# Weight blocks loaded between the parts of the memory input, their products channel by channel, and small operations queued behind later work, in a two-block transformer layer

## The chip, the cores and the metric

The kernel runs on one core of a Trainium2 chip (trn2). The metric is the device time of one execution in microseconds (us). Five engines work beside each other, each on its own queue of instructions: TensorE (PE) multiplies matrices, VectorE (DVE) and ScalarE (ACT) work element by element, GpSimd (POOL) and SyncE (SP) mainly start transfers (DMA) between the chip's memory and the core's buffers. An engine takes its instructions strictly in the order of its queue; semaphores make one engine wait for another.

## The reference

`x` (256 tokens x 1024) and a memory `mem` (256 x 1024) go through two blocks, in float32. The first block:

```python
h = rms_norm(x, norm_g); mem_h = rms_norm(mem, mem_norm_g)
(c_glu, c_gate, d_q, d_k, d_v, d_gate, x_q, x_gate, merge) = split(h @ w_in)
y_conv = conformer_conv_branch(c_glu, c_gate, ...)            # GLU, 31-tap depthwise conv, layer norm, silu, projection
y_diff = differential_attention_branch(d_q, d_k, d_v, d_gate, ...)   # 8 heads, two softmaxes subtracted
k, v = split(mem_h @ w_mem_kv); y_mem = memory_cross_attention_branch(x_q, x_gate, k, v, ...)
g = sigmoid(merge)
x = x + (g[0] * y_conv + g[1] * y_diff + g[2] * y_mem) @ w_out
```

The second block has stick-breaking attention (8 heads of 64) beside a gated linear recurrence (RG-LRU, 512 channels, whose decay is `exp(-8 r softplus(-lambda))`), a projection `w_out_2`, and a PEER feed-forward: for every token 8 heads pick 16 of 128 x 128 experts by product keys, and sum `gelu(h . u_e) v_e` over them.

## The kernel before

**The stream of weights.** All weights of both blocks are laid out as 94 blocks of 1 MB in the order of their use (`STREAM`). A block arrives as two halves `raw` (128 x 1024 each, 512 KB, five buffers) on SP's queue. `prep` (L235) loads both halves and splits each into a high part `whi` (a cast on ACT, L248) and a low part `wlo` (a subtraction on DVE, L249), four buffers each. A product with float32 accuracy then takes three matmuls (high by high, high by low, low by high), so a block is 48 matmuls of 128x256 on PE. `block` hands out a prepared block, `ahead` (L262 on) prepares exactly one block ahead. The result of a block is a tile `lin` in PSUM, three buffers. `linN` (L332 to 347) computes with the activations as the stationary side, first all channels of tokens 0 to 127, then all of tokens 128 to 255; `linT` (L309 to 311) the other way round.

**The order of the blocks.** Blocks 0 to 3 make the memory's values (`linN`), 4 to 11 the conv branch's GLU, 12 to 15 the cross attention's gate, 16 to 19 the memory's keys, 20 to 23 its queries, 24 to 31 the differential attention's queries and keys, 32 to 39 its values and the cross attention's projection, 40 to 43 its gate (`gated`, L661 on), 44 to 47 and 48 to 59 the merge gates (`merge_gate`, L674 on) and the projection between them, 60 to 67 the conv branch's end, 68 to 71 `w_out`, 72 to 81 the second block's input projection, 82 to 85 `w_out_2`, 86 to 93 the PEER queries. Behind them 64 + 64 blocks of expert matrices `u` and `v` are read whole for most tokens (L290, L1187), while the experts of 96 rows (token slots) are gathered one by one with indirect transfers from POOL (L1196, `gat`) and multiplied on DVE (L1203, L1221).

**The front** (L479 to 505). SP issues one part of the memory (`m_t`, four parts of 256 KB), the small vectors `VT`, the other three parts, the two halves of block 0, then `x` (`xr`, two halves of 512 KB), the constants `CT` and `ident`, and then the halves of the blocks from 1 on. `gain_col` (L412 to 415) makes the scaled memory `mgh` (ACT) and its low part `mgl` (DVE) for each of 8 channel groups. `rms_sq` (L437 to 441) squares two groups at a time on ACT and adds them over the channels with two matmuls against ones (8 in all) into `stat`, a PSUM tile of one buffer. `rstd_of` (L373 to 382) turns that sum into 1/sqrt in seven steps (`rv`, `rs`, `rs`, `rt` on ACT, two on DVE), and `tok_scalar` (L418 to 424) turns it into one number per token, `rmt`, by which the results of blocks 0 to 3 are scaled as they leave PSUM (`vm`, L505). Behind block 0 the program asks for the normalised input: `rms_cols` (L430) squares `x` on ACT (L393), adds on DVE (L397), sums by four matmuls into the same `stat` tile (L399), runs `rstd_of`, and makes for each of the 8 channel groups `nrm` (DVE, L409), its high part `hh` (ACT, L386) and its low part `hl` (DVE, L386). Blocks 4 to 15 need these.

**Small operations.** L511 to 517 are six DVE operations on a few columns: scaled gains (`GT`) and products (`lp`) whose first use is block 20 on, except `lp`, which a small matmul (L519) sums for `le` (L521). L769 to 775 prepare the recurrence's decay from `lambda`: on ACT `Abs`, `Exp` and `Ln` (`la`), on DVE `lb`, a sum and two scalings; first used in block 72 on. ACT needs a table load (`ACT_TABLE_LOAD`) where the next function is not in the loaded set; the one that the program loads at its start holds `Exp` and `Ln`.

**What sets the order.** The program is written in the order of use; a scheduler then orders each engine's queue from its own model of the durations. `tc.issue_after(i)` puts an operation behind `i` in that order (`hold`, `background` and `table` use it); a change in one place can so move operations elsewhere. `state["sub"]` is the latest `wlo` subtraction, `state["gate"]` the latest Sigmoid of `merge_gate`.

Of the kernel before, what the change touches and what calls it, by code (L numbers as in the profile page):

```python
# [9 lines left out]
F32 = mybir.dt.float32  # L10
# [9 lines left out]
P = 128  # L20
# [168 lines left out]
def build(tc, xT, memT, vec, con, con0, wcat, rgw, keysT, u, v, urow, vrow, out):  # L189
    nc = tc.nc  # L190
    es = ExitStack()
    with es:
# [42 lines left out]
        def prep(i):  # L235
# [4 lines left out]
            for a in range(2):  # L240
                raw = spool.tile([P, 1024], F32, name="raw", bufs=5)
                nc.sync.dma_start(raw, srcs[i][:, a * 1024:(a + 1) * 1024])
# [89 lines left out]
        def linN(act):  # L332

            ah, al = act
            hs, ls = block()
            ps = lin_ps[0].tile([P, 2, T], F32, name="lin")
            for t in range(2):
                for c in range(8):
                    wh = hs[c // 4].rearrange("p (c j) -> p c j", c=4)[:, c % 4]
                    wl = ls[c // 4].rearrange("p (c j) -> p c j", c=4)[:, c % 4]  # L340
                    xh = ah[:, c, t * P:(t + 1) * P]
                    xl = al[:, c, t * P:(t + 1) * P]
                    nc.tensor.matmul(ps[:, t], xh, wh, start=c == 0, stop=False)  # L343
                    nc.tensor.matmul(ps[:, t], xh, wl, start=False, stop=False)  # L344
                    nc.tensor.matmul(ps[:, t], xl, wh, start=False, stop=c == 7)  # L345
            ahead()
            return ps
# [118 lines left out]
        with ExitStack() as e1:  # L466
# [15 lines left out]
            nc.sync.dma_start(m_t[:, 0:2], memT[:, 0:2])  # L482
            nc.sync.dma_start(VT, vec)
            for k in range(1, 4):
                nc.sync.dma_start(m_t[:, 2 * k:2 * k + 2], memT[:, 2 * k:2 * k + 2])
            prep(0)
            for k in range(2):
                nc.sync.dma_start(x_t[:, 4 * k:4 * k + 4], xT[:, 4 * k:4 * k + 4])
            nc.sync.dma_start(CT, con)
            nc.sync.dma_start(ident, con0[:, :P])  # L490
            mgh, mgl = bigt("mgh", F32R), bigt("mgl", F32R)
            for c in range(NC):
                gain_col(m_t, "mem_norm_g", mgh, mgl, c)
            rm = smt("rm", T, 1)
            stm = statp()
# [15 lines left out]
            nc.vector.tensor_scalar_mul(GT[:, 0:1], V("diff_qn_g"), 0.125)  # L511
# [816 lines left out]
```

## Time and profile before

| what | value |
|---|---|
| three runs | 1286.37, 1287.76, 1290.27 us |
| median | 1287.76 us |
| profiled execution, its own time | 1290.27 us |
| its span | 1288.5 us (1.8 us lie around it) |
| busy, share of the span | PE 97%, DVE 73%, ACT 35%, POOL 17% |
| chain that ended last, by engine | PE 43%, issue 19%, DMA 18%, DVE 10%, POOL 6%, ACT 3% |

All times in a view count from the span's start. A row of the timeline has start, duration, engine, line, operation, output<-input, the count of equal neighbours joined in it, and in brackets how long the engine was idle before and what ended that. Durations of matmuls overlap: what one costs in a row of them is the distance between two starts. A row of the windows view sums the busy time of each engine over a stretch. The chain follows the last instruction back, at each step to what released it.

### The profile page before, as it was taken

To read this page: it belongs to the slowest core of one execution; us is meant where nothing else is said; L and a number is where in the kernel's file an instruction comes from. 1 tells how busy PE (TensorE), PEld (TensorE's weight loads), DVE (VectorE), ACT (ScalarE), POOL (GpSimd) and SP (SyncE) were. 2 spreads that over 40 slices of the span, in tenths; PEclk is the share of its full clock that TensorE was granted. 3 is DMA by queue.
4 is the path that set the end of the run, shared out by engine and by line. 5 is a ranking of instruction groups with operands and counts; after the bars stand their busy time and mean duration, and the time that the engine had idled before them with its cause. 6 is when DMAs were issued, how large, how long until landed. Compare 5 with 4: busy or idle time off the path is not lost.

```text
span 1288.5 us, 24481 instructions
## 1 busy us (share of the span) xinstructions
PE 1252.9 (97%) x9948; PEld 1211.2 (94%) x9948; DVE 936.7 (73%) x1806; ACT 457.4 (35%) x741; POOL 219.3 (17%) x232
## 2 busy tenths in 40 slices
PE   8999999999999999998999999999999999999995
PEld 7999999989999999977999999999999999999884
DVE  6789988888998776865899874678545876454542
ACT  7545677578646556964432111000100000000001
POOL 0000000000000000002013453222342225333330
PEclk9999999999999999999999999999999999999998
DMA  8555544434565664415677899999999999999994
GB/s 287 191 186 188 168 134 131 122 125 148 164 194 167 188 206 156 154 59 200 236 245 220 298 373 408 408 408 404 378 392 334 352 348 407 409 409 409 409 408 155
DMA packets 94865, 340.76 MB, mean 264 GB/s; under 512 B 10576, under 2 KB 12048, under 8 KB 94624
## 3 DMA queue, kind: packets, MB, share of 16 engines
q1 hardware_dynamic: 65312, 232.73, 51.0%
q0 software_dynamic: 29440, 106.46, 21.6%
q8 instruction: 78, 1.28, 0.4%
q14 instruction: 35, 0.29, 0.1%
HBM read 338.01 MB, written 1.05 MB: 263 GB/s over the span
## 4 chain that ended last, share of the span: by engine, by line
PE 43%; issue 19%; DMA 18%; DVE 10%; POOL 6%; ACT 3%; POOLq 0%; SPq 0%; DVEq 0%; ACTq 0%
DMA gat<-in_vrow,gi 13%; PE lin L310 10%; PE lin L309 10%; PE lin L311 10%; POOL gat L1196 5%; DMA gat<-in_urow,gi 5%; PE lin L343 1%; PE lin L345 1%; PE lin L344 1%; DVE gat L1203 1%; DVE acc L1221 1%; DVE wlo L249 1%; PE stat L461 1%; DVE s L997 1%; ACT whi L248 1%
## 5 line engine op out<-in xcount | busy, mean ns | idle before, releaser
L1187 PE MATMUL y<-ga,w 128*128 128x160 f32 x2048 | 292.9, 302 | 5.2 <-DMA w<-in_v 2.5
L1187 PEld LDWEIGHTS y<-ga,w 128*128 128x128 f32 x2048 | 279.9, 190 | 12.5 <-DMA w<-in_v 11.5
L249 DVE TENSOR_TENSOR wlo<-raw,whi 128x1024 fp32r<-128x1024 f32 x188 | 229.3, 1222 | 64.0 <-ACT whi L248 63.3
L290 PE MATMUL lin<-h3f,w 128*128 128x160 f32 x1888 | 265.4, 300 | 0.0
L290 PEld LDWEIGHTS lin<-h3f,w 128*128 128x128 f32 x1888 | 257.7, 190 | 0.2 <-issue 0.2
L248 ACT CAST whi<-raw 128x1024 fp32r<-128x1024 f32 x188 | 196.2, 1049 | 167.0 <-PE lin L310 125.7
L310 PE MATMUL lin<-hl,whi 128*128 128x256 f32 x704 | 200.2, 284 | 0.0
L311 PE MATMUL lin<-hh,wlo 128*128 128x256 f32 x704 | 199.8, 284 | 0.0
L309 PE MATMUL lin<-hh,whi 128*128 128x256 f32 x704 | 199.7, 284 | 0.0
L1221 DVE SCALAR_TENSOR_TENSOR acc<-gat,cG,acc 128x1024 f32<-128x1024 f32 x94 | 120.7, 1284 | 95.9 <-DMA gat<-in_vrow,gi 95.5
L1203 DVE CUSTOM_DVE_ANT_0 gat<-gat,hrow 128x1024 f32<-128x1024 f32 x96 | 116.1, 1223 | 28.6 <-DMA gat<-in_urow,gi 28.6
L311 PEld LDWEIGHTS lin<-hh,wlo 128*128 128x128 f32 x704 | 132.6, 188 | 2.2 <-issue 1.9
L310 PEld LDWEIGHTS lin<-hl,whi 128*128 128x128 f32 x704 | 132.6, 188 | 1.8 <-issue 1.4
L309 PEld LDWEIGHTS lin<-hh,whi 128*128 128x128 f32 x704 | 132.5, 188 | 1.4 <-issue 1.0
L1196 POOL DMA_INDIRECT gat<-in_urow,gi x96 | 101.5, 1058 | 181.2 <-DVE sG L1203 169.4
L1196 POOL DMA_INDIRECT gat<-in_vrow,gi x96 | 93.8, 977 | 166.1 <-DVE acc L1221 137.8
L1176 ACT ACTIVATE ga<-lin 128x320 f32<-128x320 f32 x64 | 28.0, 438 | 243.8 <-PE lin L290 239.5
L950 POOL DMA_DIRECT2D ga<-in_u x10 | 5.4, 545 | 601.3 <-DMA raw<-in_wcat 597.7
L537 DVE SCALAR_TENSOR_TENSOR cacc<-ub,VT,cacc 128x256 f32<-128x256 f32 x240 | 104.0, 480 | 0.0
L1302 ACT COPY ga<-y 128x160 f32<-128x160 f32 x4 | 1.2, 293 | 251.1 <-PE y L1187 251.1
L1165 DVE SCALAR_TENSOR_TENSOR ga<-gp,ga 128x256 f32<-128x256 f32 (+1 forms) x60 | 29.1, 511 | 63.3 <-PE gp L1154 55.9
L310 PE MATMUL lin<-h3lo,whi 128*128 128x256 f32 x128 | 37.6, 294 | 3.0 <-DVE h3lo L386 3.0
(376 smaller groups left out, 2152.0 us busy)
## 6 DMA issues: line engine op xcount, KB each, us to landing
raw<-in_wcat SPq DMA_DIRECT2D x188, 512.0 KB, 4.1
w<-in_v SPq DMA_DIRECT2D x128, 512.0 KB, 13.6
w<-in_u SPq DMA_DIRECT2D x118, 512.0 KB, 9.8
ga<-in_u POOLq DMA_DIRECT2D x10, 512.0 KB, 10.8
gat<-in_urow,gi POOLq DMA_INDIRECT x96, 8.9
gat<-in_vrow,gi POOLq DMA_INDIRECT x96, 18.8
m_t<-in_memT SPq DMA_DIRECT2D x4, 256.0 KB, 3.9
xr<-in_xT SPq DMA_DIRECT2D x2, 512.0 KB, 9.1
```

The costliest lines, as they stand in the source:

```text
L248: nc.scalar.copy(h, raw)
L249: state["sub"] = nc.vector.tensor_sub(l, raw, h.bitcast(F32))
L290: nc.tensor.matmul(ps[:, a], ws[a][:, c * P:(c + 1) * P], x[:, c], start=c == 0, stop=c == 7)
L309: nc.tensor.matmul(ps[:, a], wh, ah[:, c], start=(a, c) in first, stop=False)
L310: nc.tensor.matmul(ps[:, a], wh, al[:, c], start=False, stop=False)
L311: nc.tensor.matmul(ps[:, a], wl, ah[:, c], start=False, stop=(a, c) in last)
L537: nc.vector.scalar_tensor_tensor(cacc[:, c], s, w, cacc[:, c], op0=ALU.mult, op1=ALU.add)
L1165: state["dve"] = nc.vector.scalar_tensor_tensor(g_[:, :, tl], p_, 1.0 / GSCALE, g_[:, :, tl], op0=ALU.mult, op1=ALU.mult)
L1187: nc.tensor.matmul(yT[c // 2][:, c % 2, :D], ws[a][:, c * P:(c + 1) * P], g[:, a], start=False, stop=i == 63 and (a, c % 2) == (1, 1))
L1196: nc.gpsimd.indirect_dma_start(g, None, src, bass.IndirectOffsetOnAxis(gi[:, 0, k:k + 1].bitcast(U32), 0))
L1203: nc.vector.tensor_tensor_reduce(out=g, in0=g, in1=h, scale=1.0, scalar=0.0, op0=ALU.mult, op1=ALU.add, accum_out=sG[:, k:k + 1])
L1221: state["sum"] = nc.vector.scalar_tensor_tensor(acc[m], g, cG[:, k:k + 1], acc[m], op0=ALU.mult, op1=ALU.add)
```

## The change

The halves of blocks 0 and 1 are loaded among the memory's parts: SP's order becomes `VT`, part 0, block 0's first half, parts 1 and 2, block 0's second half, part 3, both halves of block 1, and only then `x`, `CT`, `ident` and the rest. The memory's statistic is squared for the first two channel groups as before (two matmuls), while the other three pairs are squared and added on DVE into one tile (two additions), with two matmuls behind block 0's products: four matmuls instead of eight. `rstd_of` and `tok_scalar` follow there. Block 0's products go channel by channel, both halves of the tokens for each; in all of `linN` the second and third product change places. The six small operations on `GT` and `lp` are put behind the latest `wlo`, `Abs` and `lb` of the decay behind the latest merge gate.

```diff
+        def prep(i, raws=None, between=None):
...
+                raw = load(i, a) if raws is None else raws[a]
+                if between is not None:
+                    between(a)
...
+            if channelwise:
+                seq = [(t, c) for c in range(8) for t in range(2)]
+                first, last = seq[:1], seq[-1:]
+            else:
+                seq = [(t, c) for t in range(2) for c in range(8)]
+                first, last = [(0, 0), (1, 0)], [(0, 7), (1, 7)]
+            for t, c in seq:
...
+                nc.tensor.matmul(ps[:, t], xh, wh, start=(t, c) in first, stop=False)
+                nc.tensor.matmul(ps[:, t], xl, wh, start=False, stop=False)
+                nc.tensor.matmul(ps[:, t], xh, wl, start=False, stop=(t, c) in last)
...
-            nc.sync.dma_start(m_t[:, 0:2], memT[:, 0:2])
             nc.sync.dma_start(VT, vec)
-            for k in range(1, 4):
-                nc.sync.dma_start(m_t[:, 2 * k:2 * k + 2], memT[:, 2 * k:2 * k + 2])
-            prep(0)
+            m_load(0)
+            raws = [load(0, 0)]
+            m_load(1)
+            m_load(2)
+            raws.append(load(0, 1))
+            m_load(3)
+            raws1 = [load(1, a) for a in range(2)]
             for k in range(2):
                 nc.sync.dma_start(x_t[:, 4 * k:4 * k + 4], xT[:, 4 * k:4 * k + 4])
...
+            stm = statp()
+            msq = [smt("sqs", 512, 1), smt("sq"), smt("sq")]
+            nc.scalar.square(msq[0].rearrange("p (a b) -> p a b", a=2), m_t[:, 0:2])
+            for b in range(2):
+                nc.tensor.matmul(stm[:, :T], ONES, msq[0][:, b * T:(b + 1) * T], start=b == 0, stop=False)
+            m_gains(0)
+            prep(0, raws, lambda a: [gain_col(m_t, "mem_norm_g", mgh, mgl, c) for c in (2, 3, 4, 5)] if a else None)
+            for c in (6, 7):
+                gain_col(m_t, "mem_norm_g", mgh, mgl, c)
+            prep(1, raws1)
+            for k in range(1, 4):
+                q = msq[min(k, 2)]
+                nc.scalar.square(q.rearrange("p (a b) -> p a b", a=2), m_t[:, 2 * k:2 * k + 2])
+                if k > 1:
+                    nc.vector.tensor_add(msq[1], msq[1], q)
...
-            for c in range(0, NC, 2):
-                rms_sq(m_t, stm, c, NC)
-            rstd_of(stm[:, :T], 1.0 / 1024, T, out=rm)
-            rmt = tok_scalar(rm, "rmt")
...
             for j in range(4):
-                ps = linN((mgh, mgl))
+                ps = linN((mgh, mgl), j == 0)
+                if j == 0:
+                    for b in range(2):
+                        nc.tensor.matmul(stm[:, :T], ONES, msq[1][:, b * T:(b + 1) * T], start=False, stop=b == 1)
+                    rstd_of(stm[:, :T], 1.0 / 1024, T, out=rm)
+                    rmt = tok_scalar(rm, "rmt")
...
-            nc.vector.tensor_scalar_mul(GT[:, 0:1], V("diff_qn_g"), 0.125)
...
+            with tc.issue_after(state["sub"].ins):
+                nc.vector.tensor_scalar_mul(GT[:, 0:1], V("diff_qn_g"), 0.125)
...
-            nc.scalar.activation(la, lam, AF.Abs)
+            with tc.issue_after(state["gate"].ins):
+                nc.scalar.activation(la, lam, AF.Abs)
             nc.scalar.activation(la, la, AF.Exp, scale=-1.0)
             nc.scalar.activation(la, la, AF.Ln, bias=1.0)
-            nc.vector.tensor_scalar(lb, lam, 0.0, -1.0, op0=ALU.min, op1=ALU.mult)
+            with tc.issue_after(state["gate"].ins):
+                nc.vector.tensor_scalar(lb, lam, 0.0, -1.0, op0=ALU.min, op1=ALU.mult)
```

The change moves instructions in three places on which the prediction rests. The line numbers of the changed kernel are higher by 6 to 40: the cast `whi` is L254 there, the low part of a split L397, `rv`, `rs`, `rs`, `rt` are L387 to L390, `vm` is L542.

**ACT, the start of the chain that makes the normalised input** (`vm` are blocks 0 to 3 leaving PSUM, `rv` to `rt` the statistic of `x`, `hh` the high parts). Before:

```order
L248 CAST whi<-raw 128x1024 x2
L505 ACTIVATE vm<-lin,rmt 128x256 x2
L248 CAST whi<-raw 128x1024 x2
L376 ACTIVATE rv<-stat,VT 128x256
L377 ACTIVATE rs<-rv 128x256
L378 ACTIVATE rs<-rs 128x256
L379 ACTIVATE rt<-rs 128x256
L248 CAST whi<-raw 128x1024
L505 ACTIVATE vm<-lin,rmt 128x256 x2
```

With the change:

```order
L254 CAST whi<-raw 128x1024 x3
L542 ACTIVATE vm<-lin,rmt 128x256 x4
L254 CAST whi<-raw 128x1024 x2
L542 ACTIVATE vm<-lin,rmt 128x256 x2
L387 ACTIVATE rv<-stat,VT 128x256
L388 ACTIVATE rs<-rv 128x256
L389 ACTIVATE rs<-rs 128x256
L390 ACTIVATE rt<-rs 128x256
L254 CAST whi<-raw 128x1024
```

`rv` stood behind one pair of `vm` (block 0's); now it stands behind three (blocks 0, 1 and 2). On PE the four matmuls that sum the squares of `x` stood inside block 1, and now stand at the end of block 2.

**PE, the end of block 46** (`hh,whi` are its products; `att<-ident,pp` are the transposes of the last differential attention head's probabilities, `sig` their copy to the core's buffers by ACT, `att<-sig,vd` the product with the values). Before:

```order
L643 MATMUL att<-ident,pp 128x128 x2
L309 MATMUL lin<-hh,whi 128x256
L310 MATMUL lin<-hl,whi 128x256
L311 MATMUL lin<-hh,wlo 128x256
...
L646 MATMUL att<-sig,vd 128x256
L647 MATMUL att<-sig,vd 128x128
```

With the change:

```order
L316 MATMUL lin<-hl,whi 128x256
L681 MATMUL att<-ident,pp 128x128 x3
L317 MATMUL lin<-hh,wlo 128x256
L684 MATMUL att<-sig,vd 128x256
L685 MATMUL att<-sig,vd 128x128
L315 MATMUL lin<-hh,whi 128x256
```

Before, the first transpose stood 28 products further ahead still, and 18 products stood between the last two transposes and the product with the values; now one does.

**ACT, the same heads a little earlier** (`gate` is the Silu of the differential attention's gate, `pp,z` the softmax, `sig` the copy after the transposes; `rv`, `rs`, `rs`, `rt` here a head norm's statistic). Before:

```order
L376 ACTIVATE rv<-stat,VT 128x512
L664 ACTIVATE gate<-lin 128x512
L377 ACT_TABLE_LOAD
L377 ACTIVATE rs<-rv 128x512
L378 ACT_TABLE_LOAD
L378 ACTIVATE rs<-rs 128x512
L572 ACTIVATE pp,z<-s,nm 128x128 x2
L379 ACTIVATE rt<-rs 128x512
L645 COPY sig<-att 128x384
```

With the change:

```order
L387 ACTIVATE rv<-stat,VT 128x512
L388 ACT_TABLE_LOAD
L388 ACTIVATE rs<-rv 128x512
L254 CAST whi<-raw 128x1024
L702 ACT_TABLE_LOAD
L702 ACTIVATE gate<-lin 128x512
L610 ACT_TABLE_LOAD
L610 ACTIVATE pp,z<-s,nm 128x128 x2
L389 ACTIVATE rs<-rs 128x512
L683 COPY sig<-att 128x384
```

Between `rv` and `pp,z` stood two table loads and no cast; now stand three and one cast.

## Rows read from the trace of the kernel before

**Rows 1.** Windows: stretch and us; busy of PE, PEld, DVE, ACT, POOL; PEclk, DMA share, GB/s.

```profile
0.00:14.40 14.40, 8.13 (x18) 5.62 (x19) 7.65 (x23) 9.99 (x20) 0.20 (x4) 1.00 0.82 281
300.00:350.00 50.00, 49.90 (x391) 48.06 (x391) 45.15 (x84) 41.30 (x63) 0.00 (x0) 1.00 0.51 159
550.00:600.00 50.00, 47.42 (x357) 41.27 (x356) 26.56 (x44) 24.62 (x38) 1.81 (x4) 1.00 0.27 83
725.00:1250.00 525.00, 518.44 (x4218) 509.01 (x4218) 323.34 (x519) 24.81 (x60) 186.67 (x183) 1.00 0.99 385
```

**Rows 2.** The chain that ended last, its longest pieces: start, us, what.

```profile
2.62 6.30 DMA m_t<-in_memT
...
10.42 2.08 PE stat L441 x4
12.71 1.71 PE stat L441 x4
...
1168.04 18.80 DMA gat<-in_vrow,gi
```

**Rows 3.** Timeline of SP's queue, first us: issue of block 0's two halves.

```profile
3.09 0.91 SPq L242 DMA_DIRECT2D raw<-in_wcat  x2
```

**Rows 4.** DMA issues of the stretch 3.4 to 3.8 us: KB each, us to landing.

```profile
raw<-in_wcat SPq DMA_DIRECT2D x2, 512.0 KB, 7.5
```

**Rows 5.** Timeline of PE, blocks 0, 1 and the start of 4.

```profile
12.51 1.91 PE L441 MATMUL stat<-sq,ONES 128*128 128x256 f32 x4
...
14.43 0.41 PE L345 MATMUL lin<-whi,mgl 128*128 128x256 f32 x1
14.64 0.32 PE L343 MATMUL lin<-whi,mgh 128*128 128x256 f32 x1
...
19.84 0.28 PE L344 MATMUL lin<-wlo,mgh 128*128 128x256 f32 x1
19.96 0.28 PE L345 MATMUL lin<-whi,mgl 128*128 128x256 f32 x1
20.17 0.60 PE L422 MATMUL stat<-ONES,rm 1*128 1x1 f32 x4
20.70 0.39 PE L343 MATMUL lin<-whi,mgh 128*128 128x256 f32 x1
...
22.24 1.02 PE L399 MATMUL stat<-sqs,ONES 128*128 128x256 f32 x4
...
39.08 0.36 PE L309 MATMUL lin<-hh,whi 128*128 128x256 f32 x1
39.28 0.28 PE L310 MATMUL lin<-hl,whi 128*128 128x256 f32 x1
```

**Rows 6.** Timeline of DVE, the front.

```profile
12.89 1.22 DVE L249 TENSOR_TENSOR wlo<-raw,whi 128x1024 fp32r<-128x1024 f32 x1 [0.24 <-ACT whi L248]
...
26.41 0.88 DVE L409 SCALAR_TENSOR_TENSOR nrm<-xr,VT,rs 128x256 f32<-128x256 f32 x2
...
39.97 0.75 DVE L386 TENSOR_TENSOR hl<-nrm,hh 128x256 fp32r<-128x256 f32 x2
```

**Rows 7.** Timeline of ACT, the front.

```profile
5.70 0.19 ACT L769 ACTIVATE la<-VT 128x4 f32<-128x4 f32 x1
5.80 0.89 ACT L414 ACTIVATE mgh<-m_t,VT 128x256 fp32r<-128x256 f32 x2
...
21.73 1.99 ACT L248 CAST whi<-raw 128x1024 fp32r<-128x1024 f32 x2
23.62 0.48 ACT L376 ACTIVATE rv<-stat,VT 128x256 f32<-128x256 f32 x1
```

**Rows 8.** Timeline of ACT, blocks 46 and 47.

```profile
326.24 0.62 ACT L386 CAST odh<-gate 128x512 fp32r<-128x512 f32 x1 [0.93 <-DVE gate L665]
...
328.26 0.48 ACT L645 COPY sig<-att 128x384 f32<-128x384 f32 x1
328.76 1.28 ACT L676 ACT_TABLE_LOAD   x1
330.05 0.60 ACT L676 ACTIVATE sig<-lin 128x512 f32<-128x512 f32 x1
```

**Rows 9.** Timeline of PE, the same stretch.

```profile
327.84 0.38 PE L643 MATMUL att<-ident,pp 128*128 128x128 f32 x2
...
330.17 0.59 PE L646 MATMUL att<-sig,vd 128*128 128x256 f32 x2
```

**Rows 10.** Timeline of ACT around the last merge gate of that kind.

```profile
386.88 1.06 ACT L248 CAST whi<-raw 128x1024 fp32r<-128x1024 f32 x1 [1.76 <-PE lin L310]
```

More of the change, by code (lines that the diff above doesn't have):

```diff
@@ L233, in prep_plain, with load @@
             prepared[i] = ws
-        def prep(i):
+        def load(i, a):
+            raw = spool.tile([P, 1024], F32, name="raw", bufs=5)
+            nc.sync.dma_start(raw, srcs[i][:, a * 1024:(a + 1) * 1024])
+            return raw
+        def prep(i, raws=None, between=None):
             if i >= NW:
@@ L330, in linK, with linN @@
                 yield ps
-        def linN(act):
+        def linN(act, channelwise=False):
             ah, al = act
@@ L336, in linN @@
             ps = lin_ps[0].tile([P, 2, T], F32, name="lin")
[L337 to L345, printed above, removed]
+            if channelwise:
[5 more added lines that the diff above has]
+            for t, c in seq:
+                wh = hs[c // 4].rearrange("p (c j) -> p c j", c=4)[:, c % 4]
+                wl = ls[c // 4].rearrange("p (c j) -> p c j", c=4)[:, c % 4]
+                xh = ah[:, c, t * P:(t + 1) * P]
+                xl = al[:, c, t * P:(t + 1) * P]
+                nc.tensor.matmul(ps[:, t], xh, wh, start=(t, c) in first, stop=False)
+                nc.tensor.matmul(ps[:, t], xl, wh, start=False, stop=False)
+                nc.tensor.matmul(ps[:, t], xh, wl, start=False, stop=(t, c) in last)
             ahead()
@@ L481, in build, with m_load, m_gains @@
             m_t = bigt("m_t")
-            nc.sync.dma_start(m_t[:, 0:2], memT[:, 0:2])
+            def m_load(k):
+                nc.sync.dma_start(m_t[:, 2 * k:2 * k + 2], memT[:, 2 * k:2 * k + 2])
             nc.sync.dma_start(VT, vec)
-            for k in range(1, 4):
-                nc.sync.dma_start(m_t[:, 2 * k:2 * k + 2], memT[:, 2 * k:2 * k + 2])
-            prep(0)
+            m_load(0)
[5 more added lines that the diff above has]
+            raws1 = [load(1, a) for a in range(2)]
             for k in range(2):
                 nc.sync.dma_start(x_t[:, 4 * k:4 * k + 4], xT[:, 4 * k:4 * k + 4])
+            mgh, mgl = bigt("mgh", F32R), bigt("mgl", F32R)
+            def m_gains(a):
+                for c in range(4 * a, 4 * a + 2):
+                    gain_col(m_t, "mem_norm_g", mgh, mgl, c)
[7 more added lines that the diff above has]
+            for c in (6, 7):
+                gain_col(m_t, "mem_norm_g", mgh, mgl, c)
+            prep(1, raws1)
[4 more added lines that the diff above has]
+                    nc.vector.tensor_add(msq[1], msq[1], q)
+            rm = smt("rm", T, 1)
             nc.sync.dma_start(CT, con)
             nc.sync.dma_start(ident, con0[:, :P])
[L491 to L495, printed above, removed]
-            for c in range(0, NC, 2):
-                rms_sq(m_t, stm, c, NC)
-            rstd_of(stm[:, :T], 1.0 / 1024, T, out=rm)
-            rmt = tok_scalar(rm, "rmt")
             vm = big.tile([P, 2, 1024], F32, name="vm", tag="big")
```

14 lines of the change are left out of this document (6 added, 8 removed).

## The prediction

> **What bounds the kernel now.** I read the windows first. Over the middle of the first block PE is busy for 49.90 of 50 us, in the long last stretch for 518.44 of 525 with the DMA engines at 0.99, and only two stretches leave it idle: the first 14.4 us, where it works 8.13, and the stretch around `w_out_2`, 47.42 of 50 [rows 1]. A gain must therefore come out of the front, and anything that makes PE wait in between is paid in full. Then the chain of waits: it begins with the memory's transfer (6.30 us from 2.62) and runs through the passes of its statistic on PE, 2.08 and 1.71 us; at the far end it hangs on single gathers of 18.80 us [rows 2]. These start only when the second block has chosen its experts, so I take everything behind the PEER queries as shifted rigidly with what comes before: a microsecond that PE gains or loses earlier is a microsecond at the end.
>
> The timeline of PE shows what a block is: from 19.84 to 19.96 the spacing of products is 0.12, so 48 of them take 5.7 to 5.8; block 1 starts at 20.70, block 4 at 39.08 [rows 5]. From 39.08 on, products are 0.117 apart, so block 4 ends at 39.08 + 48 x 0.117 = 44.7. The first spacing, 14.43 to 14.64, is 0.21 [rows 5]: PE is slower when it comes out of an idle front, although the granted clock reads 1.00 [rows 1].
>
> **Front, the gain.** Before, the first seven transfers are `VT`, four parts and block 0's two halves; the change has the same seven first, in another order. The halves were issued until 3.09 + 0.91 = 4.00 [rows 3] and land 7.5 later [rows 4], so the seven are in at about 11.4; now the last of them is part 3, and block 0's second half (one part of 256 KB of 2.2 MB in all earlier) is in at some 10.8, an estimate. Its cast takes 1.0 (a pair 1.99 [rows 7]) and its low part 1.22 [rows 6]: 13.0. Channel by channel, the first 24 products run beside that, the last 24 follow: 24 x 0.12 = 2.9, to 15.9, or 24 x 0.21 = 5.0, to 18.0, if PE is still slow. Two of the statistic's matmuls follow (four cost up to 1.02 [rows 5], and those fp32 passes twice that while slow). Block 1 so starts between 16.8 and 20.6, the later end if the gains of part 3 (two pairs of 0.89 on ACT [rows 7]) come late. I take 17.7: a gain of 20.70 - 17.7 = 3.0, bounds 0 and 3.9.
>
> **Front, where it goes.** What block 4 needs is the normalised input, and that chain is not earlier but later in the queues. Before, four matmuls for the statistic of `x` stood in block 1, at 22.24 [rows 5], and `rv` ran at 23.62 [rows 7]. In the changed order they stand at the end of block 2, and `rv` on ACT behind two more pairs of `vm`. Block 2 ends at 17.7 + 2 x 5.8 + 0.5 for the small `rmt` matmuls (0.60 [rows 5]) = 29.8. ACT then has two casts for block 4 whose buffers block 2 releases (1.99 [rows 7]) ahead of `rv`, and a pair of `vm`, part of it already running: `rv` at about 31.5. From `rv` to the first `nrm` it took 26.41 - 23.62 = 2.8 [rows 6, 7]: 34.3. From there DVE makes eight `nrm` of 0.44 and eight `hl` of 0.38, with two `wlo` of 1.22 between [rows 6]: 8 x 0.82 + 2.44 = 9.0, and some 0.6 of hand-overs to ACT's `hh`: the last `hl` ends at 43.9, where it ended at 39.97 + 0.75 = 40.7 [rows 6]. In the new order block 4 alternates the channels, so only some seven products, 0.8, stand behind it: block 4 ends at 44.7, exactly as before. So this term is **0**: the gain of 3.0 turns into waits inside block 4. Bounds: -3.0, if DVE and ACT take this chain between their casts without loss, and +2.5, the chain starting late by as much.
>
> **Two extra additions on DVE, four matmuls fewer, six small operations moved.** DVE has the additions where it worked 7.65 of 14.4 us [rows 1]; the matmuls are in the sum above; the small operations cost some 0.15 each by the nearest row, the 0.19 of `la` [rows 7], and now stand ahead of the statistic's two last steps: at most 6 x 0.19 = 1.1, and they stand there while `rv` to `rt` run on ACT. Zero.
>
> **The decay's operations.** ACT's `Abs`, `Exp`, `Ln` go behind the last of the merge gates at 386 to 388, where the set of Sigmoid is loaded: three loads of 1.28 [rows 8] and three operations of 0.19 [rows 7], 4.4 us. ACT's casts wait 1.76 there each for PE to release a buffer [rows 10], and a whole block (5.6 us of PE) is prepared ahead. I cost it at zero; without that cover up to 3.84. The DVE operation `lb` hardly moves, since its gate is an instruction of ACT.
>
> **The middle, blocks 44 to 47.** The scheduler has shifted the last differential heads. Before, the last transposes ran at 327.84 and the product with the values at 330.17 [rows 9], 18 products later. Under those 18 ACT did the copy at 328.26, the load at 328.76 and the Sigmoid at 330.05 [rows 8], which frees a `lin` buffer. Now one product stands between. From the transposes: 0.42 to the copy, the copy 0.48, the cast `odh` 0.62, the load 1.28, the Sigmoid 0.60 [rows 8, 9] = 3.4. PE meanwhile has the transposes, a product and the product with the values, 0.14 + 0.12 + 0.57 = 0.8, and then must have one of three `lin` buffers for block 47, all held by blocks 44 to 46. It waits about **2.5**. Bounds 0.7 (only the copy is waited for) and 3.4. A little earlier, ACT has one more table load, 1.28, and one more cast, 1.06, ahead of `pp`: between 0 and 2.9, and I take **0.5**, near the covered end, since PE's queue has products to put in front.
>
> Every load in this sum counts 1.28: the one at 328.76 ends at 330.04 and the Sigmoid starts at 330.05 [rows 8]. The Trainium skill, page "ScalarE: Activation LUTs", section "What ACT_TABLE_LOAD costs", puts about 1.38 us of draining beside that, 2.66 us in all for each switch. The trace does not show it here: nothing lies between the load and its Sigmoid. By that figure the middle would cost some 1.4 more and the sum would be 4.7 instead of 3.3, an estimate from that page.
>
> **Late, `w_out_2`.** One low part there stands behind one more `wlo`, 1.22 [rows 6]; PE idles 2.6 of 50 there already [rows 1], so there is little cover, but the casts ahead can also come sooner. I take **+0.3**, bounds -1.2 and +1.2.
>
> **Sum.** 0 + 2.5 + 0.5 + 0 + 0.3 = +3.3. Against the profiled execution's 1290.27 that is 1293.6; this execution lies 2.5 above the median of the runs, 1287.76, so in the terms of the median: **1291.1 us**. A measurement of this kernel can tell some 0.3%, 3.9 us, from no change: faster means below 1283.9, slower above 1291.6.
>
> **Rivals.**
> - *The chain of the normalised input is hidden.* For it: ACT and DVE have free time in the front, and part of the gain of 3.0 is only handed to DVE. Against: DVE's 9.0 us are a straight sum. Then front -2.5, sum +0.8: 1288.6. Chance 0.17.
> - *Slower than before: slow products through block 0.* PE stays at 0.21 (48 x 0.09 = 4.3 over a block), or the halves land late, so that block 2 ends 2.5 later than 29.8. Since the chain hangs on the end of block 2 and DVE's work behind it can't shrink, each of these microseconds goes to the end from the point at which block 2 ends after 29.8: +2.5, sum +5.8, 1293.6. For it: the spacing at 14.43 [rows 5]. Against: PE sped up within two products there. Chance 0.15. This is also the case in which the early loading does not do what it says. The Trainium skill, page "TensorE: Matmul & The Clock Gate", section "What's actually happening", has the array start at 1.2 GHz and reach 2.4 GHz once it has been busy; the spacing agrees, the column of the granted clock does not show it.
> - *The decay's loads are on the path,* 3.8 more: 1294.9. Against: the 1.76 of idle time before each cast [rows 10]. Chance 0.08.
> - *Front kept and the middle hidden,* -3.0 to -3.9 + 0.3: about 1284.8. For it: waits of ACT have been covered by the scheduler in many other places. Chance 0.10, half of it faster.
>
> **How the numbers follow.** The forecast has 0.48, its own range 1289.5 to 1292.9 (0.27 of it within 0.3%, 0.21 slower). With the rivals: within 0.3% 0.27 + 0.17 + 0.05 = 0.49; slower 0.21 + 0.15 + 0.08 + 0.01 of the rest = 0.45; faster 0.05 + 0.01 = 0.06. The range reaches from the middle of the bounds of the kept front, 1286.0, to the loads on the path, 1295.5; the last rival and the rest lie mostly outside.
>
> **What would show it.** Block 1 at 17.7 (gain) and `rv` of `x` at 31.5 instead of 23.62, the last `hl` at 43.9, PE waiting inside block 4 for `hl`, block 5's start within half a microsecond of 44.7; around the end of block 46 a hole of 2.5 on PE, ended by ACT's copy and Sigmoid; no hole at the decay's loads; every later stage shifted by the same amount. The prediction is wrong if block 5 starts at 42 or at 47, if there is no hole after block 46, or if the later stages are shifted by another amount than block 48.

## The result, and the profile after

Six runs of the changed kernel took 1296.59 to 1304.14 us, median 1301.72; six runs of the kernel before 1284.99 to 1290.27, median 1288.72. The ratio is 1.0104, interval [1.0084, 1.0124]: **slower by about 13 us**. The profiled execution took 1304.14 us (span 1302.4), 13.9 more than the one shown of before; each is the slowest of its six.

Where the time went is read from the start of each stage. The lines view of the changed kernel (line, engine, operation, count, least/median/largest ns, first and last start in us):

```profile
L315 PE MATMUL lin<-mgh,whi x64: 277/281/283, 109.4 to 132.6; 128*128 128x256 f32 x64
L354 PE MATMUL lin<-whi,hh x64: 277/282/685, 223.2 to 280.2; 128*128 128x256 f32 x64
L315 PE MATMUL lin<-h2h,whi x128: 277/281/682, 489.2 to 542.0; 128*128 128x256 f32 x128
L315 PE MATMUL lin<-h3hi,whi x128: 277/281/415, 619.1 to 676.3; 128*128 128x256 f32 x128
L296 PE MATMUL lin<-h3f,w x1888: 297/299/403, 676.6 to 982.3; 128*128 128x160 f32 x189
```

and the same view of the kernel before:

```profile
L309 PE MATMUL lin<-mgh,whi x64: 277/280/283, 106.7 to 130.0; 128*128 128x256 f32 x64
L343 PE MATMUL lin<-whi,hh x64: 277/282/685, 220.4 to 277.3; 128*128 128x256 f32 x64
L309 PE MATMUL lin<-h2h,whi x128: 277/280/682, 479.6 to 532.2; 128*128 128x256 f32 x128
L309 PE MATMUL lin<-h3hi,whi x128: 277/281/416, 606.8 to 663.8; 128*128 128x256 f32 x128
L290 PE MATMUL lin<-h3f,w x1888: 297/299/403, 664.2 to 967.6; 128*128 128x160 f32 x189
```

Block 16 starts 2.7 late, block 32 2.8, block 72 (`h2h`) 9.6, the PEER queries (`h3hi`) 12.3, the expert matrices 12.4, and the end is 13.9 late. So there are three places: **the front (2.7), the middle between blocks 32 and 72 (6.8), the end of the second block's attention (2.7)**; behind them the shift is nearly rigid.

The windows of the changed kernel, answering to [rows 1] and then, in pieces of 5 us, around the three places:

```profile
0.00:14.40 14.40, 6.78 (x27) 5.59 (x28) 6.49 (x14) 8.98 (x16) 0.20 (x4) 1.00 0.85 299
300.00:350.00 50.00, 46.01 (x358) 44.30 (x357) 39.88 (x76) 38.59 (x61) 0.00 (x0) 0.97 0.45 145
550.00:600.00 50.00, 48.68 (x367) 41.48 (x367) 27.76 (x44) 29.11 (x48) 0.00 (x0) 1.00 0.28 92
725.00:1250.00 525.00, 518.80 (x4225) 510.96 (x4224) 329.34 (x555) 27.89 (x64) 186.91 (x183) 0.99 0.99 383
...
40.00:45.00 5.00, 4.91 (x26) 4.70 (x27) 4.80 (x13) 2.41 (x6) 0.00 (x0) 0.66 0.50 172
335.00:340.00 5.00, 2.87 (x13) 2.63 (x14) 5.00 (x9) 4.46 (x8) 0.00 (x0) 0.78 0.67 214
340.00:345.00 5.00, 5.00 (x34) 4.52 (x34) 4.32 (x9) 2.51 (x4) 0.00 (x0) 0.88 0.28 96
610.00:615.00 5.00, 5.00 (x16) 4.07 (x17) 1.73 (x3) 1.76 (x3) 2.81 (x6) 0.66 0.86 261
```

Before, at the middle place:

```profile
335.00:340.00 5.00, 5.00 (x44) 5.00 (x43) 5.00 (x12) 4.78 (x6) 0.00 (x0) 1.00 0.48 149
```

The middle's 49.90 of PE have become 46.01, where the last long stretch is as before (518.80). At each of the three places the granted clock is below 1.00: PE first waits, then works a while at the lower of its two levels (1.2 instead of 2.4 GHz), so a full busy column there hides slow work.

**The front.** PE, ACT and DVE of the changed kernel's timeline; they answer to [rows 5 to 7]:

```profile
37.30 0.48 PE L315 MATMUL lin<-hh,whi 128*128 128x256 f32 x2
38.50 0.39 PE L316 MATMUL lin<-hl,whi 128*128 128x256 f32 x1 [0.72 <-DVE hl L397]
32.52 0.51 ACT L387 ACTIVATE rv<-stat,VT 128x256 f32<-128x256 f32 x1
44.23 0.82 DVE L397 TENSOR_TENSOR hl<-nrm,hh 128x256 fp32r<-128x256 f32 x2
```

Block 4 starts at 37.30 instead of 39.08, so the early loading does gain; but `rv` runs at 32.52 instead of 23.62, the last `hl` ends at 45.05 instead of 40.7, and PE waits for low parts (`hl`) inside block 4.

**The middle.** Waits of PE between 318 and 340 us, where the kernel before has none (engine, line, whom it waits for: us in total, times, longest):

```profile
PE att L684 <- ACT sig L683: 2.5, 2, 1.4
PE lin L315 <- ACT sig L714: 1.5, 1, 1.5
```

The timeline at the end of block 46, PE and ACT; it answers to [rows 8, 9]:

```profile
333.95 0.49 PE L681 MATMUL att<-ident,pp 128*128 128x128 f32 x3
334.19 0.36 PE L317 MATMUL lin<-hh,wlo 128*128 128x256 f32 x1
335.62 0.70 PE L684 MATMUL att<-sig,vd 128*128 128x256 f32 x2 [1.07 <-ACT sig L683]
338.05 0.58 PE L315 MATMUL lin<-hh,whi 128*128 128x256 f32 x1 [1.51 <-ACT sig L714]
338.65 0.41 PE L317 MATMUL lin<-hh,wlo 128*128 128x256 f32 x1
338.86 0.41 PE L315 MATMUL lin<-hh,whi 128*128 128x256 f32 x1
335.10 0.47 ACT L683 COPY sig<-att 128x384 f32<-128x384 f32 x1
335.47 0.62 ACT L397 CAST odh<-gate 128x512 fp32r<-128x512 f32 x1
336.11 1.28 ACT L714 ACT_TABLE_LOAD   x1
337.40 0.60 ACT L714 ACTIVATE sig<-lin 128x512 f32<-128x512 f32 x1
```

This is the predicted chain: transposes, copy, cast, load, Sigmoid, and PE waiting at both ends. The load ends at 337.39 and its Sigmoid starts at 337.40. Behind the wait the products stand 0.21 apart, not 0.12.

**The end of the attention.** Waits of PE between 600 and 624 us:

```profile
PE lin L316 <- DVE h3lo L397: 3.0, 1, 3.0
PE stat L452 <- ACT sq L450: 2.0, 1, 2.0
PE lin L315 <- ACT h3hi L397: 1.6, 1, 1.6
```

Before, the first and third are there unchanged, and the statistic waits 1.5. The chain names the passes behind that wait; before:

```profile
599.15 3.91 PE stat L441 x16
```

after:

```profile
609.95 5.42 PE stat L452 x16
```

### The profile page after: what moved, and what is told of

The parts are those of the page before. It is cut to its first block, busy times and chain, and to the rows that moved or that the text cites. A ratio compares the mean times of both kernels' runs of the same rounds, so it can differ in the third digit from the quotient of the medians.

```text
span 1302.4 us, 24471 instructions
## 1 busy us (share of the span) xinstructions
PE 1258.8 (97%) x9940; PEld 1217.2 (93%) x9940; DVE 937.5 (72%) x1808; ACT 462.4 (36%) x745; POOL 219.8 (17%) x232
## 3 DMA queue, kind: packets, MB, share of 16 engines
q1 hardware_dynamic: 65312, 232.73, 50.3%
## 4 chain that ended last, share of the span: by engine, by line
PE 42%; issue 19%; DMA 18%; DVE 10%; POOL 6%; ACT 4%; POOLq 0%; SPq 0%; DVEq 0%; ACTq 0%
DMA gat<-in_vrow,gi 13%; PE lin L315 10%; PE lin L316 10%; PE lin L317 10%; POOL gat L1236 6%; DMA gat<-in_urow,gi 5%; PE lin L356 1%; PE lin L354 1%; PE lin L355 1%; DVE wlo L255 1%; ACT whi L254 1%; DVE acc L1261 1%; DVE gat L1243 1%; PE stat L472 1%; PE lin L296 1%
## 5 line engine op out<-in xcount | busy, mean ns | idle before, releaser
L254 ACT CAST whi<-raw 128x1024 fp32r<-128x1024 f32 x188 | 195.9, 1048 | 165.1 <-PE lin L316 127.6
## 6 DMA issues: line engine op xcount, KB each, us to landing
w<-in_v SPq DMA_DIRECT2D x128, 512.0 KB, 12.3
```

The costliest lines, as they stand in the source:

```text
L254: nc.scalar.copy(h, raw)
```

## Experiments

Seventeen kernels ran. A ratio is to the kernel before, from runs on one chip.

### Which edit makes the middle and the late loss

**e1_small_only.** The kernel before with the small operations moved and nothing else:

```diff
-            nc.vector.tensor_scalar_mul(GT[:, 0:1], V("diff_qn_g"), 0.125)
+            with tc.issue_after(state["sub"].ins):
+                nc.vector.tensor_scalar_mul(GT[:, 0:1], V("diff_qn_g"), 0.125)
...
+            with tc.issue_after(state["gate"].ins):
+                nc.scalar.activation(la, lam, AF.Abs)
```

> The kernel before with only the small operations put behind later work (GT and lp behind the latest subtraction, the decay's Abs and lb behind the latest merge gate); the front as before. Theory 1 (all the time is lost where PE waits, at three places that the front's edit has re-ordered, and again behind each while PE runs at half clock): no place is touched, so within 2 us of the kernel before, and no new wait on PE, although ACT has three table loads more. Rival 2 (the queued small operations cost it: three table loads on ACT at the merge gates, six operations ahead of the chain of x): 3.8 to 13 us slower than before.

Measured: 1.0007 [0.9997, 1.0016]. No new wait of PE appears. Moving them costs nothing that can be told.

**e2_front_only.** The reverse: the changed kernel with these operations back in their places (the same lines with - and + exchanged).

> The changed kernel with the small operations put back to where they stood before; the front's loads, the products channel by channel and the statistic stay. Theory 1: as slow as the changed kernel, some 13 us over before (10 to 15), with the same shifts: block 6 about +2.5 to +3, block 50 about +8, the second block's statistic +12. Rival 2: at most 5 over before.

Measured: 1.0087 [1.0074, 1.0101], block 16 2.2 late, block 48 7.1. The loss lies in the other half of the diff.

**e4_after_mid.** The changed kernel; block 46's last 18 products are issued behind the last transposes, as they stood before.

```diff
+                            state["tr"] = nc.tensor.transpose(pt[:, o:o + P], pp[:, 0, kb * P:(kb + 1) * P], ident)
...
+                    if behind is not None and 3 * n >= behind[0]:
+                        s.enter_context(tc.issue_after(behind[1].ins))
...
+                nc.vector.tensor_mul(yj, yj, merge_gate(j, behind=(30, state["tr"]) if j == 2 else None))
```

> The changed kernel, with the last 18 products of block 46 issued behind the last head's transposes, so that on PE they stand between the transposes and the product with the values as they did before; their inputs are ready in the changed kernel 7 us before PE reaches them. Theory 1: the two waits behind block 46 (1.3 and 1.6 us) and the half clock from 338 to 342 (some 2.4 us) go, the earlier wait at 321.9 (1.6 us) stays: block 50 at about +3.5 to +4.5 against before instead of +8.8, in all 4 to 5 us faster than the changed kernel. Rival 4 (ACT is simply behind there, with its extra table load and cast, and PE will wait for it anyway): block 50 at +7 or more.

Measured: 1.0075 [1.0058, 1.0091]. Of the two waits behind block 46 both are gone; left between 318 and 345 us:

```profile
PE att L687 <- ACT sig L686: 1.4, 1, 1.4
PE att L684 <- DVE od L477: 0.4, 1, 0.4
```

Block 48 is 4.2 late instead of 8.8; less the front of each (2.2 and 2.65), this place with its slow products cost 8.8 - 2.65 - (4.2 - 2.2) = 4.1. Some of it comes back as a new wait of 0.9, ended at 485.7.

**e5_swap_only.** The kernel before with only the second and third product of `linN` exchanged. The arithmetic and the instruction count are the same.

```diff
-                    nc.tensor.matmul(ps[:, t], xh, wl, start=False, stop=False)
-                    nc.tensor.matmul(ps[:, t], xl, wh, start=False, stop=c == 7)
+                    nc.tensor.matmul(ps[:, t], xl, wh, start=False, stop=False)
+                    nc.tensor.matmul(ps[:, t], xh, wl, start=False, stop=c == 7)
```

> The kernel before with one edit: in linN the second and third product of each channel change places, nothing else. The same work in the same number of products, but the scheduler answers with the changed kernel's order in the differential attention's heads (last transposes one product ahead of the product with the values, 28 table loads). Theory 5 (the middle's and the late loss come from this exchange alone, by the order that it sets off): block 4 as before (within 0.3), block 60 at +4.5 to +7 against before with waits behind block 46, the second block's statistic at +6 to +10: 6 to 10 us slower than before. Rival 6 (the middle waits because the front has shifted the stages or moved x): within 2 us of before.

Measured: **1.0059 [1.0043, 1.0074]**, 1296.28 against 1288.08 us. Its waits between 318 and 340, and that of the statistic:

```profile
PE att L646 <- ACT sig L645: 2.5, 2, 1.4
PE lin L309 <- ACT sig L676: 1.5, 1, 1.5
...
PE stat L441 <- ACT sq L439: 2.0, 1, 2.0
```

They are the changed kernel's waits to a tenth. Two lines that do the same work in another order let the scheduler reorder the differential heads in blocks 44 to 47 and the `w_out_2` stage; the loads, the channel order and the small operations have no part in it.

**e6_after_oldorder.** The changed kernel with the old order of products wherever the block is not taken channel by channel.

```diff
+                for x, w in ((xl, wh), (xh, wl)) if channelwise else ((xh, wl), (xl, wh)):
```

> The changed kernel with the old order of the three products in linN wherever it does not go channel by channel (all blocks but block 0). Theory 5: the middle and the late part as before, only the front's +2.2 to +2.8 stays: 2 to 4 us slower than before, 10 faster than the changed kernel. Rival 6: still 8 us or more over before.

Measured: 1.0027 [1.0016, 1.0037]. Block 16 is 1.7 late, and the shift stays between 2.0 and 2.3 up to the expert matrices: the front alone. The parts add up: 0.0059 (e5) + 0.0027 (e6, in which the small operations are moved too) = 0.0086, just inside the change's interval.

**e10_swap_late.** The kernel before, the exchange only in blocks 80 and 81 (`linN(h2, True)`).

> The kernel before with the second and third product exchanged in linN for the second block's two value blocks (80, 81) alone. If the exchange's late part (+1.1 between 550 and 593 us, and a longer wait ahead of the statistic) comes from these two blocks: no shift up to 540 us, then +1 to +1.5, and up to +2 more where the passes run at half clock: 1 to 3.5 slower than before. If it is a consequence of the middle: within 0.7.

Measured: 1.0027 [1.0016, 1.0038], about 3.5 us, a wait of 2.0 ahead of the statistic. So in the exchange the middle and the late place share about evenly, by the medians (0.0027 of 0.0059).

### What the front's loss hangs on

**e3_after_xstat.** The changed kernel; the statistic of `x` gets a PSUM tile of its own, so that it need not follow the memory's.

```diff
-            rms_cols(x_t, "norm_g", hh, hl)
+            rms_cols(x_t, "norm_g", hh, hl, ps=sq_sum(x_t, NC, attp()))
```

> The changed kernel, with the statistic of x summed in a PSUM tile of its own instead of the one that the memory's statistic and its per-token copy use; its four matmuls then stand 87 products into the stream instead of 144, inside block 1. Theory 1: PE's waits inside block 4 go, and the half clock behind them: block 6 at -2 to -2.5 against before where the changed kernel has +3, the two later places unchanged, so 4 to 6 us faster than the changed kernel, some 8 slower than before. Rival 3 (the late chain of x is bound by its data or by DVE's work, not by its place in the queues): block 6 stays at +1 or later, within 1.5 us of the changed kernel.

Measured: 1.0065 [1.0050, 1.0081]. `rv` moves from 32.52 to 25.11, the last `hl` from 45.05 to 42.80, and block 16 starts 0.7 earlier than before instead of 2.7 later. The middle waits are unchanged. `rv`, which now reads the tile `att`:

```profile
25.11 0.47 ACT L387 ACTIVATE rv<-att,VT 128x256 f32<-128x256 f32 x1 [0.29 <-PE att L410]
```

**e7_xstat_oldorder.** e3 and e6 together.

> Both repairs: the old order of products outside block 0, and the statistic of x in a PSUM tile of its own. Theories 1 and 5: the front's shift is the -0.7 of the run with that statistic, nothing is added behind: 0.3 to 1.5 us faster than before, which the measurement can hardly tell from no change. If the two places interact, slower than before by more than 1.

Measured: 1.0010 [1.0000, 1.0020]. With both repairs the loss is gone, and nothing is gained.

**e11_front_repaired** is e7 without the move of the small operations, **e12_x_first** is e11 with block 1's halves behind `x` again:

```diff
-            raws1 = [load(1, a) for a in range(2)]
             for k in range(2):
                 nc.sync.dma_start(x_t[:, 4 * k:4 * k + 4], xT[:, 4 * k:4 * k + 4])
+            raws1 = [load(1, a) for a in range(2)]
```

> The front of the change with both repairs (x's statistic in its own PSUM tile, the old order of products outside block 0) and the small operations where they stood before. With the front's -0.7 to -1.6 kept to the end: 0.5 to 2 us faster than before. If the run with the small operations (1.0010) shows all there is to have: within 1 us of before.

> The same, with the two halves of x loaded ahead of block 1's halves instead of behind them. If x's data set the chain's start: the last low part some 1 us earlier, block 6 at -2 to -3 against before, 1.5 to 3 us faster than before. If block 1's weights come late in exchange: PE waits ahead of block 1, and the gain is as without it or less.

Measured: 1.0010 [1.0001, 1.0019] and 1.0005 [0.9995, 1.0016]. The new front with its chain repaired gains nothing that can be told, with `x` behind block 1 or ahead of it.

**e15_after_high_first_4.** The changed kernel; block 4's 32 products with the high part of the activations (`hh`) are issued first, its 16 with the low part (`hl`) last.

```diff
-                pb = linT(h)
+                pb = linT(h, j == 0, j == 0)
```

> The changed kernel with the products of block 4 in that order: high parts first, low parts last. If the front's loss is PE's wait for the low parts of x: block 6 some 1.5 to 2.5 us earlier than in the changed kernel, the time 1.5 to 3 less. If the chain's end sets it (the last low part at 45 us, and few products behind it): the same time as the changed kernel within 1 us.

Measured: 1.0085 [1.0061, 1.0108], block 16 at 108.09, 1.35 late instead of 2.65: a little ahead of the six draws of the changed front below, far from repaired, and no help in the median.

Since a front starts with transfers, it varies from execution to execution. All profiles of three fronts (e12 and e15 have fronts of their own), in us: the start of the 48th recorded product of block 0, and of block 16.

| front | kernels | 48th product | block 16 |
|---|---|---|---|
| as before | before | 19.96 | 106.75 |
| as before | e1, e5, e10, e13, e17 | 17.57 to 19.29 | 104.35 to 106.07 |
| as changed | after, e2, e4, e6, e8, e9 | 17.26 to 18.88 | 108.49 to 110.22 |
| statistic of `x` apart | e3, e7, e11, e14, e16 | 16.24 to 18.39 | 103.86 to 106.06 |

The profile of before was the slowest of six draws. On the means (18.83 and 105.75 before, 17.95 and 109.14 changed) block 0 ends 0.9 earlier, and block 16 starts 3.4 later.

### What the lower clock is worth

**e8_after_fill** is the changed kernel with four matmuls of constants into an unused tile ahead of the second block's statistic; **e9_fill_both** has six more between block 46's last product and the product with the values. Their results go nowhere.

```diff
+            fl = attp()
+            with tc.issue_after(state["kmm"].ins):
+                for k in range(4):
+                    nc.tensor.matmul(fl[:, :T], ONES, CT[:, :T], start=True, stop=True)
```

> The changed kernel with four more matmuls (ones times constants, 128x256 in float32, into a PSUM tile that nobody reads) issued behind the last product of the second block's output projection, so that PE works through the wait of 2.30 us ahead of the second block's statistic. Work added: some 1.7 us. Clock theory (a part of the late loss is not the wait but PE at half clock behind it): the eight passes of the statistic come at 0.21 instead of 0.43 and the shift there drops by 1.5 to 2 us, in spite of more work. Rival 7 (the passes are slow because of what feeds them): passes at 0.43, the time unchanged or up to 1.7 us longer.

> The changed kernel with work that nobody needs put into two of its waits on PE: the four matmuls ahead of the second block's statistic, and six more (ones times constants, 2.6 us in all) between block 46's last product and the product with the values, where the changed kernel waits 1.3 and then 1.6 us. Clock theory (a wait of PE is paid twice, once itself and once as half clock behind it): the granted clock reads 1.00 in both stretches behind, products of block 47 at 0.12 and the statistic's passes at 0.21, and with 10 matmuls more in the program it is 2 to 5 us faster than the changed kernel (some 8 to 11 over before). Without that: the same shifts as the changed kernel or up to 3 us slower.

Measured: 1.0075 [1.0061, 1.0089] and 1.0082 [1.0068, 1.0096]. In e9's profile the clock is granted in full at both places, with matmuls in the place of most of the idle time:

```profile
335.00:340.00 5.00, 4.75 (x29) 4.20 (x28) 5.00 (x10) 4.74 (x8) 0.00 (x0) 1.00 0.59 206
```

and e5, with equal waits and no fill, shows

```profile
335.00:340.00 5.00, 5.00 (x26) 4.52 (x25) 4.53 (x11) 1.90 (x4) 0.00 (x0) 0.66 0.47 155
```

So the fill holds the clock in these profiles. But the clock is also 1.00 in that stretch in e2, which has the waits and no fill:

```profile
335.00:340.00 5.00, 3.26 (x23) 3.02 (x24) 5.00 (x10) 4.07 (x7) 0.00 (x0) 1.00 0.73 218
```

In the changed kernel the clock can take at most 5 x (0.22 + 0.12) = 1.7 us behind block 46. What it does take is read across the profiles that have the changed order and, but for e9, the same waits in the middle (2.5 and 1.5); before, block 48 starts 122.62 us after block 32:

| profiles | granted clock, 335 to 340 and 340 to 345 us | block 32 to block 48, longer by |
|---|---|---|
| e2, e3, e15 | 1.00, 1.00 | 4.7, 4.5, 4.6 |
| e9 (filled) | 1.00, 1.00 | 4.7 |
| after | 0.78, 0.88 | 6.0 |
| e5 | 0.66, 1.00 | 6.1 |
| e8 | 0.66, 0.66 | 7.2 |

At the late place, behind the same wait of 2.0, the sixteen passes of the statistic take 5.42 to 5.44 in the changed kernel, e2, e3 and e15, and 3.91 in e4, e5 and e10; with the fill, in e8 and e9, 3.91 too. So the lower clock costs 1.3 to 2.6 us in the middle and 1.5 late where it comes, and after equal waits it comes in some executions and not in others.

In the medians neither e8 nor e9 separates from the change (1.0104 [1.0084, 1.0124]). The mean granted clock of every execution is on record too: 0.987 to 0.993 in the six of the changed kernel (the slowest, the one profiled, has 0.987, the fastest, 1296.59 us, 0.993), 0.993 to 0.996 in the five of e9, 0.991 to 0.996 in 84 of the kernel before. From the medians, 0.9905 and 0.993, comes an estimate of 0.0025 x 1302 = 3.3 us of the 13 for a typical execution, if PE has work throughout.

### A better version

The kernel before already has a hole of 3.0 in block 86, where PE waits for `h3lo`. **e13_high_first** is the kernel before with block 86's 32 high-part products first and its 16 low-part products last:

```diff
-                pq = linT(h3, hd == 0)
+                pq = linT(h3, hd == 0, hd == 0)
```

> The kernel before with one edit: in block 86, the first that waits for the second block's normalised output, the 32 products with the high part go first and the 16 with the low part behind them. PE waited 3.36 us there and then ran at half clock (granted 0.50 from 610 to 615). Without the clock: the wait goes, up to 3 us faster than before, less what PE must still wait for the high parts. With the clock theory: the half clock goes too, 4 to 6 us faster. If DVE's low parts were the bound all the same, or a later stage takes it back: within 1 us.

Measured: 0.9992 [0.9975, 1.0008], its runs in two groups, 1284.5 to 1287 and 1290.5 to 1293. In the profile the `h3lo` wait is gone, and a new one stands behind it:

```profile
PE gp L1085 <- DMA kT<-in_keysT: 5.7, 1, 5.7
...
608.60 10.26 POOL L968 COPY xG<-xr 128x768 f32<-128x768 f32 x1
618.88 0.33 SPq L982 DMA_DIRECT2D kT<-in_keysT  x1
```

SP issues the keys `kT` at 618.88, just after POOL's copy of a residual `xG` has ended (608.60 + 10.26 = 618.86). In the profile of before that copy took

```profile
608.67 0.83 POOL L966 COPY xG<-xr 128x768 f32<-128x768 f32 x1
```

**e14_best** puts the same edit on e11, **e16_best_copy_on_act** adds the copy on ACT, and **e17_before_high_first_copy_on_act** is e13 with the copy on ACT behind the statistic:

```diff
-        nc.gpsimd.tensor_copy(xG, xr[:, :, D:])
+        with tc.issue_after(state["rstd"][0].ins):
+            nc.scalar.copy(xG, xr[:, :, D:])
```

> The repaired front (e11) with the same order of products in block 86. e11 was 1.0010: if the two add, its time less what e13 gains; this is the version that should beat both kernels if e13 does.

> e14 (repaired front, high parts first in block 86) with the copy of the gathered tokens' rows on ACT behind the statistic's square instead of on POOL. If POOL's copy gave the gain back in some executions: 2 to 4 us faster than before, with a narrower spread. If what e14 lacks lies in the later stages: as e14, 1 to 2 us faster than before.

> e13 (the kernel before with the high parts first in block 86) with the same copy on ACT. If POOL's copy was what split e13's times into two groups (1284.5 to 1287 and 1290.5 to 1293): only the faster group, 2 to 4 us faster than before. Otherwise still two groups.

Measured: 0.9990 [0.9978, 1.0002], 0.9995 [0.9986, 1.0004], and **0.9970 [0.9958, 0.9982]**: e17, 1284.81 against 1288.40 us, beats both kernels. Its seven runs, 1284.4 to 1287.13, lie where e13's faster group lies, as they should if POOL's copy made the slower one. Its window there:

```profile
605.00:610.00 5.00, 4.36 (x36) 4.36 (x37) 5.00 (x15) 4.82 (x10) 0.87 (x2) 1.00 1.03 412
610.00:615.00 5.00, 5.00 (x43) 4.83 (x42) 5.00 (x7) 4.96 (x7) 0.00 (x0) 1.00 1.02 422
```

against the kernel before:

```profile
605.00:610.00 5.00, 0.60 (x3) 0.19 (x1) 4.93 (x11) 2.95 (x8) 2.42 (x4) 0.86 1.01 397
610.00:615.00 5.00, 4.81 (x22) 4.81 (x23) 5.00 (x12) 4.03 (x5) 0.00 (x0) 0.50 1.03 423
```

PE works 4.36 of 5 us where it worked 0.60, and then at the full clock where it had half. On the changed front (e14, e16) the same edits do not show beyond the measurement. Their profiles gain there too (from block 86 to the expert matrices e14 takes 4.5 us less than the profile of before, e16 and e17 5.4 less), so why the times do not follow stays open.

## Why the prediction was wrong

The forecast was 1291.1; the median is 1301.72, beyond the range.

- **The front was forecast at 0 and cost about 3** (2.65 in the profile, 3.4 on the means). In the profile block 1 starts at 18.12, near the forecast's 17.7; but the base, 20.70, came from the slowest of six draws, so 1.1 of the gain of 3.0 was that draw, and on the means about 0.9 is left. The mechanism that takes it back, the normalised input's chain, was right, and e3 shows it: with the statistic in its own tile the loss is gone. Its size was off: `rv` came at 32.52 instead of 31.5, the last `hl` at 45.05 instead of 43.9. "Only some seven products stand behind it" had the place wrong: PE's order alternates the first halves of blocks 4 and 5, and by the trace 34 of their 96 products had been issued when the last `hl` was done (41 in e2, whose clock is 1.00 there and not 0.66). The other 62 x 0.117 = 7.3 end at 52.3, where the forecast's 44.7 with block 5's 48 x 0.117 behind it comes to 50.3. That is 2.0 of the 2.65. The last 0.65, up to block 16, has no wait: from 46 to 100 us the products stand 0.1187 apart on the mean, in the profile of before 0.1173, at a granted clock of 1.00 in both, which makes 480 x 0.0014 = 0.7. The change is not the cause of that: e1, with the old front, has 0.1187, and e4, with the new one, 0.1173. Its cause stays open.
- **The middle was forecast at 3.0 and cost 6 to 7 in the profile** (6.0 up to block 48, of which the lower clock is about 1.4; 4.1 by the medians, e5 less e10). The place, the chain and the mechanism were right. The term of 2.5 at the end of block 46 measured 1.07 + 1.51 = 2.6. The "0.5, near the covered end" for the earlier head measured 1.4: PE had nothing to put in front there. And no term stood for what follows a wait: products at half the clock. The Trainium skill, page "TensorE: Matmul & The Clock Gate", section "HAM oscillation — how this bites in real kernels", says of a kernel whose matmuls wait for transfers that each wait throws the array back to its lower clock, so that the next work starts slow. This trace agrees behind the 1.51 (products 0.21 apart, granted 0.78), e2's does not with the same waits. The prediction used that page for the front alone.
- **Late was forecast at 0.3 and cost about 3.** By e10 it is 0.0027, 3.5 us; in the changed kernel's profile the statistic waits 2.0 instead of 1.5, and its passes take 5.42 instead of 3.91. The passes are the lower clock, which e10's own profile does not have there (3.91): in it, blocks 80 to 86 take 1.1 longer, so part of the 3.5 is not placed. The step had looked for a low part behind one more `wlo`; what moved was the `w_out_2` stage as the exchange reorders it.
- **The cause in common was never costed.** The part-by-part list has no line for "the second and third product change places". I treated it as neutral because the count and the kind of the products do not change. Its effect was read off the order as "the scheduler has shifted the last differential heads", and put down to the change as a whole. e5 shows that this one exchange makes over half of the loss.
- **Right were the zeros:** the small operations and the decay's loads (e1: 1.0007), and the load without a drain (337.39 to 337.40). The rigid shift behind the PEER queries holds to 1.5 us (12.4 at the expert matrices, 13.9 at the end).
- **The rivals:** none is what happened. "Slow products through block 0" had the sign and not the mechanism: its products do stand 0.21 apart from 10.87 to 13.43 (and 0.12 behind that), yet block 0 was earlier. Of the rivals for a slower kernel each moved one term; none had two misses of the same sign together. The ends of the range, 1286.0 and 1295.5, do not come out of the prediction's own figures (the loads on the path give 1294.9), and even its upper bounds for the front, the middle and the late place, 2.5 + 3.4 + 2.9 + 1.2 = 10.0, reach only 1297.8.

## What to carry to other kernels

Where a scheduler orders the queues, an edit that changes no work can cost more than the transfers it rides along with: an exchange of two equal products cost 0.59%, so list each edit of a diff apart and time it apart. A wait of the bound engine may be paid twice, once as idle time and once as slow work behind it, as in 3 of 6 profiles in the middle and 4 of 7 late; read the granted clock of the next stretch, in several profiles. The front of a single profile is one draw, here 17.6 to 20.0 us for the same point, so a gain below that spread needs several profiles.

## What was not expected of the hardware

The same POOL copy of 128x768 took 0.83 us in 15 of 17 profiles, 7.0 in e9 and 10.26 in e13; the long ones made nothing late in e9 and held up the keys in e13. The Trainium skill, page "GPSIMD Engine Reference", section "1. Specifications", says that GpSimd shares its interfaces to the core's buffers with VectorE, and that some of VectorE's instructions contend for them; DVE is busy for 5.00 of 5 us there in e9, but that it is the cause was not tried. And the granted clock after equal waits is not the same from execution to execution: behind block 46 it was 0.78 in the changed kernel, 0.66 in e5 and e8, 1.00 in e2 and e3.
